# The attention norm's factor spread by a DRAM round trip, later rotary products, and a 128-wide first FoX block

## The chip, the cores and the metric

One Trainium2 chip, one core. The time is that of one execution on the device, in microseconds (us): from the first to the last instruction of the program with what lies around it. The kernel before takes 1466.55 us, the median of three runs (1466.13 to 1466.87).

## The reference, cut to what matters

Two decoder layers on x, 512 tokens of width 1024, all float32. A layer normalizes x by its root mean square, projects it, runs two attention mixers over it (FoX, eight heads with a forget term; NSA, eight heads with compressed, selected and window branches, queries and keys partly rotated), mixes them, and ends in an MLP behind a second norm.

```python
def rmsnorm(x, g):
    y = xf * lax.rsqrt(jnp.mean(xf * xf, axis=-1, keepdims=True) + RMS_EPS)
    return (y * g).astype(x.dtype)
...
    h = rmsnorm(x, norm_mix)
    proj = h @ w_in
    q_a, k_a, v_a, f_a, q_b, kv_b, g_b, gate_a, gate_b = jnp.split(proj, ...)
...
        s = jnp.einsum('bhqd,bhkd->bhqk', qi, k) * scale      # FoX, 128 queries at a time
        s = s + ci[..., :, None] - c[..., None, :]
        s = jnp.where(kpos[None, :] <= qpos[:, None], s, -jnp.inf)
...
    q_n = partial_rope(to_heads(q_b, NSA_HEADS), pos)
    ks = partial_rope(ks, pos)
    kw = partial_rope(kw, pos)
```

## The kernel before, in words

Every product of float32 numbers is made of three matmuls on numbers split into a high and a low part (fp32r): high by high, high by low, low by high. Weights come by DMA from the SyncE queue into `raw`; `convert` (L175 to L192) splits them, the high part `wh` by a copy on ScalarE (L189), the low part `wl` by a subtraction on VectorE (L190). All activations lie transposed, features on the partitions and tokens along the row, and x is multiplied by the norm's gain but not by the norm's factor before the projections. The factor, one number for each token, is put on each projection's result instead. It is needed in two forms:

- `rc`, [128, 4]: the factor of token 128 b + p in partition p, column b. The projections with tokens on the partitions use it (`vf`, L806 and L807; `vn`, `z`, `th`, L819 to L824).
- `R`, [128, 512]: the factors of all 512 tokens along the row, the same in every partition. The projections with tokens along the row use it: `scaled` (L344) for FoX's keys and queries, the two rotary tables `CRS` (L829 to L832), which `roped` (L334 to L340) multiplies with the NSA queries and keys, and the gates (L915).

`rstd` (L266) makes both: four matmuls sum the squares over the partitions (L273), a few small operations of VectorE and ScalarE make `rc` (L276 to L284), then four matmuls of `rc`'s columns with the identity write `R` into a PSUM bank (L289), and ScalarE copies it to SBUF (L294). `layer` (L781) calls it once a layer, between the value projection (`va`) and the second small projection (`g2`), and lets two steps of the projection go between the last small operation and the four matmuls.

In each layer the stages around it are: the value projection and `g2` (`token_proj`, in four chunks of weights each), the forget term (`forget`), the first pair of FoX heads (`fox_proj(0)`), then `attend` over the eight FoX units. A unit's `scores` (L404) makes, for each of four blocks of 128 queries, the scores against the keys up to that block, with two matmuls of 128 queries (L429 and L432); the first block has 128 keys that count and takes 256 columns, `w = max(n, 256)`. Between the units' matmuls stands the work of a generator, `fill1` (the other projections of FoX, the compression, the NSA keys and queries).

The order on each engine comes from a scheduler in the framework: it orders the program's instructions by its own costs and by what they depend on, each engine then takes its list in that order, and waits at an instruction whose inputs are not there. Only the MLP's order is pinned.

Of the kernel before, what the change touches and what calls it, by code (L numbers as in the profile page):

```python
# [19 lines left out]
T = 512  # L20
# [122 lines left out]
class Body:  # L143
# [119 lines left out]

        self.nc.scalar.activation(self.t("s4", [128, 1], name="warm"), after[:, :1], f)

    def rstd(self, acc, tags=("O", "O"), wait=iter(()), exp=True, copy=True):  # L266

        nc = self.nc
        n = acc[0].shape[-1] // 128
        ps = self.p(tags[0])  # L270
        for b in range(n):
            for i, t in enumerate(acc):
                nc.tensor.matmul(ps[:, 2 * b:2 * b + 2], t[:, b * 128:(b + 1) * 128],  # L273
                                 self.ones2, start=i == 0, stop=i == len(acc) - 1)
        v, s, y, z = (self.t("s4", [128, NB], name=k)[:, :n] for k in "vsyz")
        nc.vector.tensor_scalar(v, ps[:, 0:2 * n:2], 1.0 / D, 1e-6, op0=OP.mult, op1=OP.add)  # L276
        nc.scalar.activation(s, v, AF.Sqrt)
        if exp:
            self.table(AF.Exp, s)
        nc.vector.reciprocal(y, s)  # L280
        nc.vector.tensor_mul(z, y, y)
        nc.vector.scalar_tensor_tensor(z, z, -0.5, v, op0=OP.mult, op1=OP.mult)
        rc = self.t("g4", [128, NB], name="rcol")[:, :n]
        nc.vector.scalar_tensor_tensor(rc, z, 1.5, y, op0=OP.add, op1=OP.mult)  # L284
        for _ in range(2):
            next(wait, None)
        ps = self.p(tags[1])[:, :128 * n]
        for b in range(n):
            nc.tensor.matmul(ps[:, b * 128:(b + 1) * 128], rc[:, b:b + 1].to_broadcast([128, 128]), self.ident,  # L289
                             start=True, stop=True)  # L290
        if not copy:
            return ps, rc
        R = self.t("r", [128, T], name="R")[:, :128 * n]
        nc.scalar.copy(R, ps)  # L294
        return R, rc


# [106 lines left out]
    def scores(self, u):  # L404
        nc = self.nc
        q, k = u["q"](), u["k"]()
        E = self.t("e", [128, 1280], name="E")
        sm = u.get("sm")
        if sm is None:
            sm = self.t("s4", [128, NB], name="sm")  # L410
        u["E"] = u.get("E", [])

        def probs(e, ps, sm, i):
            n = 128 * (i + 1)
            mx = self.t("s4", [128, 1], name="mx")
            with self.tc.high_priority(20):
                nc.vector.tensor_tensor_reduce(e, ps, self.mask[:, T - n:], -1.0, BIG, OP.add, OP.min, mx)  # L417
                nc.scalar.activation(e, e, AF.Exp, bias=mx, scale=-1.0, accum_out=sm[:, i:i + 1])  # L418

        for i in range(len(u["E"]), NB):  # L420
            n = 128 * (i + 1)
            w = max(n, 256)
            ps = self.p("S")
            qs = q[:, i * 128:(i + 1) * 128]
            keys = k[:, :, :w]
            mate = u.get("mate") if i == 0 else None
            if mate is not None:
                keys = u["kk"]()
            nc.tensor.matmul(ps[:, :w], qs, keys[:, 0], start=True, stop=False)  # L429
            if "qx" in u:  # L430
                qs = u["qx"]()[:, i * 128:(i + 1) * 128]
            nc.tensor.matmul(ps[:, :w], qs, keys[:, 1], start=False, stop=True)  # L432
            e = E[:, 64 * i * (i + 1):64 * (i + 1) * (i + 2)]
            probs(e, ps[:, :n], sm, i)
            u["E"].append(e)
            if mate is not None:
                e = self.t("e0", [128, 128])
                mate["sm"] = self.t("s4", [128, NB], name="sm")
                probs(e, ps[:, 128:256], mate["sm"], 0)
                mate["E"] = [e]  # L440
            yield
        r = self.t("s4", [128, NB], name="rr")
        nc.vector.reciprocal(r, sm)
        if "gate" in u:
            nc.vector.tensor_mul(r, r, u["gate"]())
        for i in range(NB):
            e = u["E"][i]
            if i > 0:
                nc.vector.tensor_scalar(e, e, r[:, i:i + 1], None, op0=OP.mult)
            else:  # L450
                nc.scalar.activation(e, e, AF.Copy, scale=r[:, i:i + 1])  # L451
# [329 lines left out]
    def layer(self, l, u):  # L781
# [8 lines left out]
        for i in range(6 if l else 8):  # L790
            next(g)
            if l and i == 2:
                self.acc = self.late()
        self.R, self.rc = R, rc = self.rstd(self.acc, ("O", "O"), wait=g)
        if l:
            self.pinned()
        run(g)
# [28 lines left out]
        nc.vector.tensor_scalar(gt, th.rearrange("p b (h c) -> p b c h", c=3), 0.5, 0.5, op0=OP.mult, op1=OP.add)  # L826
        for b in range(NB):
            nc.vector.tensor_scalar(gt[:, b, 0], gt[:, b, 0], self.const("rowv")[:, b:b + 1], None, op0=OP.mult)
        self.CRS = self.t("crs", [128, 2, T])  # L829
        nc.sync.dma_start(self.CRS, a["rope"])  # L830
        for i in range(2):
            nc.vector.tensor_tensor(self.CRS[:, i], self.CRS[:, i], R, op=OP.mult)  # L832
        self.forget(z.rearrange("p b h -> p (b h)"))

        st = {}
# [30 lines left out]
            yield from self.cmp_probs(hk)  # L866

        def fill1():
            yield from fox_proj(1)
            yield from proj(8, "kc", self.scaled)  # L870
            yield from proj(9, "vc", self.scaled)
            c = self.compress(st["kc"], st["vc"], small, l)
            self.kk = self.t("crs", [128, 2, 2, 2, 128], F32R, name="kk")
            rest = chain(fox_proj(2), fox_proj(3), proj(10, "ks", lambda ps: self.k_pair(self.roped(ps), branch=0)),
                         proj(11, "kw", lambda ps: self.k_pair(self.roped(ps), branch=1)), qproj(0), qproj(1))
            yield from alternate(c, rest)
# [220 lines left out]
    def go(self):  # L1097
        nc, a = self.nc, self.a
        self.gain = self.cp.tile([128, 40], F32, name="gain")
        nc.scalar.dma_start(self.gain, a["gain"])  # L1100
        self.ones2 = self.cp.tile([128, 2], F32, name="ones")
        nc.vector.memset(self.ones2, 1.0)
        ones = self.t("tmp", [128, 128], name="ones")
        nc.vector.memset(ones, 1.0)
        ps = self.p("PT")
        for _ in range(self.WARM):
            nc.tensor.matmul(ps[:, :128], ones, ones, start=True, stop=True)
        warm = self.t("s4", [128, 1], name="warm")
        nc.scalar.activation(warm, ones[:, :1], AF.Exp)
        self.xs, self.xr = ([self.dp.tile([128, T], F32, name=f"{n}{k}") for k in range(KT)] for n in ("xs", "xr"))  # L1110
        self.x_src = [a["xT"][k] for k in range(KT)]
        self.acc, u = [], []
        self.plan = deque(x for l in range(L) for x in self.order(l))
        self.loaded, self.split = deque(), deque()
        self.raws = deque(("e", "e"))
        for l in range(L):
            u = self.layer(l, u)
            self.x_src = self.xs
# [703 lines left out]
```

## Time and profile before

| | before |
|---|---|
| median of 3 runs | 1466.55 us (1466.13 to 1466.87) |
| the profiled execution's own time | 1466.06 us |
| its span, first to last instruction | 1464.3 us |
| TensorE (PE) busy | 1450.4 us, 99% |
| VectorE (DVE) busy | 1205.9 us, 82% |
| ScalarE (ACT) busy | 916.7 us, 63% |
| GpSimd (POOL) busy | 146.6 us, 10% |
| granted TensorE clock | 0.998 of 2.4 GHz |

PE is TensorE's matmuls, PEld its weight loads. A matmul's duration in the trace runs over its neighbours (matmuls are pipelined), so what one costs is read from the distance between starts. Layer 0's norm stands near 30 us of the span, layer 1's near 748 us.

### The profile page before, as it was taken

How to read it: one execution, taken by the hardware profiler on the slowest of the kernel's cores; microseconds unless marked ns; L12 is line 12 of the kernel's file. 1: busy time of each engine (PE TensorE's matmuls, PEld its weight loads, DVE VectorE, ACT ScalarE, POOL GpSimd, SP SyncE). 2: the span in 40 equal slices, each digit the busy share in tenths (PEclk: the TensorE clock that was granted, in tenths of full speed). 3: DMA queues.
4: the chain of work that ended last, by engine and by line, in shares of the span. 5: the costliest groups of instructions: out<-in, count | busy, mean ns of one | idle time of the engine just before them, and what ended most of it. 6: DMA issues, size and time to landing. Idle time of an engine off the chain costs nothing.

```text
span 1464.3 us, 23475 instructions
## 1 busy us (share of the span) xinstructions
PE 1450.4 (99%) x8312; PEld 1261.2 (86%) x8312; DVE 1205.9 (82%) x2490; ACT 916.7 (63%) x1886; POOL 146.6 (10%) x199
## 2 busy tenths in 40 slices
PE   9999999999999999999999999999999999999997
PEld 8877888888898999989888788888888989899896
DVE  6587988777789898989866779887787888989897
ACT  6375666664577575848454657666646776757584
POOL 2000100000011111111300001000000111111113
PEclk9999999999999999999999999999999999999999
DMA  7564522126447676777836644221353475766774
GB/s 255 168 158 135 151 87 65 66 73 201 137 113 181 176 175 183 177 171 214 255 133 166 178 114 126 87 72 59 97 177 101 118 176 154 185 176 175 180 192 115
DMA packets 79477, 216.72 MB, mean 148 GB/s; under 512 B 10112, under 2 KB 10496, under 8 KB 79360
## 3 DMA queue, kind: packets, MB, share of 16 engines
q1 hardware_dynamic: 59104, 164.08, 35.3%
q0 software_dynamic: 17664, 46.67, 17.5%
q10 hardware_dynamic: 2592, 4.48, 0.8%
q8 instruction: 65, 1.06, 0.3%
q14 instruction: 52, 0.43, 0.1%
HBM read 168.46 MB, written 6.29 MB: 119 GB/s over the span
## 4 chain that ended last, share of the span: by engine, by line
PE 94%; DVE 3%; ACT 2%; issue 1%; DMA 0%; POOL 0%; ACTq 0%; DVEq 0%
PE ps_mm L215 10%; PE ps_mm L216 10%; PE ps_mm L217 9%; PE ps_mm L1530 7%; PE ps_S L1530 7%; PE ps_mm L1403 6%; PE ps_PT L1403 6%; PE ps_S L1403 6%; PE ps_O L485 4%; PE ps_PT L464 4%; PE ps_O L1403 3%; PE ps_O L1530 3%; PE ps_PT L1530 3%; PE ps_S L429 2%; PE ps_S L432 2%; PE ps_O L575 1%
## 5 line engine op out<-in xcount | busy, mean ns | idle before, releaser
L215 PE MATMUL ps_mm<-uh,wh 128*128 128x512 f32 x480 | 191.3, 398 | 0.2
L216 PE MATMUL ps_mm<-ul,wh 128*128 128x512 f32 x480 | 189.2, 394 | 0.0
L217 PE MATMUL ps_mm<-uh,wl 128*128 128x512 f32 x480 | 188.4, 392 | 0.0
L189 ACT CAST wh<-raw 128x1024 fp32r<-128x1024 f32 (+2 forms) x111 | 112.6, 1015 | 88.1 <-PE ps_mm L216 50.3
L1512 ACT CAST sh<-raw 128x512 fp32r<-128x512 f32 x160 | 96.7, 620 | 78.0 <-DVE raw L1611 26.8
L190 DVE TENSOR_TENSOR wl<-raw,wh 128x1024 fp32r<-128x1024 f32 (+2 forms) x111 | 130.5, 1177 | 17.2 <-ACT wh L189 17.1
L418 ACT ACTIVATE E<-E,mx 128x512 f32<-128x512 f32 (+3 forms) x176 | 101.3, 576 | 48.9 <-DVE mx L417 48.0
L468 ACT CAST pth<-ps_PT 128x512 fp32r<-128x512 f32 x144 | 73.2, 514 | 76.1 <-PE ps_PT L464 75.5
L1520 DVE TENSOR_TENSOR sl<-raw,sh 128x512 fp32r<-128x512 f32 x160 | 106.2, 684 | 12.1 <-ACT sh L1512 11.8
L417 DVE CUSTOM_DVE_ANT_0 E<-ps_S,ct 128x512 f32<-128x512 f32 (+3 forms) x176 | 87.3, 501 | 30.6 <-PE ps_S L432 29.8
L469 DVE TENSOR_TENSOR ptl<-ps_PT,pth 128x512 fp32r<-128x512 f32 x144 | 84.7, 597 | 33.3 <-ACT pth L468 31.8
L217 PEld LDWEIGHTS ps_mm<-uh,wl 128*128 128x128 f32 x480 | 90.2, 188 | 18.5
L215 PEld LDWEIGHTS ps_mm<-uh,wh 128*128 128x128 f32 x480 | 90.3, 188 | 15.6 <-DVE tmp L337 0.8
L216 PEld LDWEIGHTS ps_mm<-ul,wh 128*128 128x128 f32 x480 | 90.4, 188 | 13.6
L1377 POOL DMA_DIRECT2D raw<-raw x32 | 28.0, 874 | 734.8 <-DVE sl L1370 194.5
L1356 ACT CAST sh<-raw 128x512 fp32r<-128x512 f32 x128 | 74.6, 618 | 37.0 <-DMA raw<-raw 29.9
L1370 DVE TENSOR_TENSOR sl<-raw,sh 128x512 fp32r<-128x512 f32 x128 | 84.0, 685 | 10.8 <-ACT sh L1356 10.7
L1403 PE MATMUL ps_S<-t,sh 128*128 128x256 f32 x384 | 83.0, 282 | 0.0
L464 PE MATMUL ps_PT<-ct,E 128*128 128x128 f32 x464 | 76.3, 275 | 0.9 <-ACT E L451 0.6
L1356 ACT CAST sh<-sx 128x512 fp32r<-128x512 f32 x96 | 58.4, 615 | 28.7 <-DVE sx L1338 24.7
L1403 PE MATMUL ps_S<-t,sl 128*128 128x256 f32 x256 | 72.0, 281 | 0.0
L1370 DVE TENSOR_TENSOR sl<-sx,sh 128x512 fp32r<-128x512 f32 x96 | 64.5, 686 | 8.0 <-ACT sh L1356 7.7
(452 smaller groups left out, 4406.4 us busy)
## 6 DMA issues: line engine op xcount, KB each, us to landing
raw<-wb SPq DMA_DIRECT2D x64, 512.0 KB
raw<-wup SPq DMA_DIRECT2D x64, 512.0 KB
raw<-wt POOLq DMA_DIRECT2D x48, 512.0 KB, 6.6
raw<-wt SPq DMA_DIRECT2D x32, 512.0 KB
sx<-wt SPq DMA_DIRECT2D x64, 256.0 KB
kd<-hl SPq DMA_DIRECT2D x40, 256.0 KB
w<-w SPq DMA_DIRECT2D x32, 256.0 KB
raw<-wo SPq DMA_DIRECT2D x16, 512.0 KB
```

Source lines behind the costliest of these rows:

```text
L189: nc.scalar.copy(h[:, :n], raw[:, :n])
L190: nc.vector.tensor_tensor(lo[:, :n], raw[:, :n], h[:, :n].bitcast(F32), op=OP.subtract)
L215: mm(ps, h[:, c], xh, start=start and i == 0, stop=False)
L216: mm(ps, h[:, c], xl, start=False, stop=False)
L217: mm(ps, lo[:, c], xh, start=False, stop=stop and i == ks - 1)
L418: nc.scalar.activation(e, e, AF.Exp, bias=mx, scale=-1.0, accum_out=sm[:, i:i + 1])
L464: nc.tensor.transpose(ps[:, j * 128:(j + 1) * 128], E[i][:, b * 128:(b + 1) * 128], self.ident)
L1356: self.nc.scalar.copy(h, self.source(k, i))
L1370: self.nc.vector.tensor_tensor(lo, self.source(k, i), h.bitcast(F32), op=OP.subtract)
L1403: self.nc.tensor.matmul(ps, w, x, skip_group_check=True, **kw)
L1520: self.nc.vector.tensor_tensor(lo, self.operand(d, i, p), h.bitcast(F32), op=OP.subtract)
L1530: self.nc.tensor.matmul(ps[t][:, cols], a[:, s], m, start=new and f == 0, stop=f == 2, skip_group_check=True)
```

## The change

`rstd` no longer makes `R` with matmuls. It writes `rc` to a small DRAM tile `row` of [4, 128] by a DMA from POOL's queue, turned so that the 512 factors stand in a row, and reads that row back into all 128 partitions of `R` by a second DMA from the same queue. Second, `CRS` is allocated and its two products with `R` are written in `fill1`, the load before FoX's second pair of projections and the products behind it. Third, FoX's first block of scores is 128 columns wide, not 256; NSA's stays at 256.

```diff
@@ rstd @@
-    def rstd(self, acc, tags=("O", "O"), wait=iter(()), exp=True, copy=True):
+    def rstd(self, acc, tag="O", wait=iter(()), exp=True):
...
         nc.vector.scalar_tensor_tensor(rc, z, 1.5, y, op0=OP.add, op1=OP.mult)
+        nc.gpsimd.dma_start(self.row.rearrange("b p -> p b"), rc)
         for _ in range(2):
             next(wait, None)
-        ps = self.p(tags[1])[:, :128 * n]
-        for b in range(n):
-            nc.tensor.matmul(ps[:, b * 128:(b + 1) * 128], rc[:, b:b + 1].to_broadcast([128, 128]), self.ident,
-                             start=True, stop=True)
-        if not copy:
-            return ps, rc
-        R = self.t("r", [128, T], name="R")[:, :128 * n]
-        nc.scalar.copy(R, ps)
+        R = self.t("r", [128, T], name="R")
+        nc.gpsimd.dma_start(R, self.row.rearrange("b p -> (b p)")[None, :].to_broadcast([128, T]))
         return R, rc
@@ scores @@
-            w = max(n, 256)
+            w = max(n, 256) if "qx" not in u else n
@@ layer @@
-        self.CRS = self.t("crs", [128, 2, T])
-        nc.sync.dma_start(self.CRS, a["rope"])
-        for i in range(2):
-            nc.vector.tensor_tensor(self.CRS[:, i], self.CRS[:, i], R, op=OP.mult)
...
         def fill1():
+            self.CRS = self.t("crs", [128, 2, T])
+            nc.sync.dma_start(self.CRS, a["rope"])
             yield from fox_proj(1)
+            for i in range(2):
+                nc.vector.tensor_tensor(self.CRS[:, i], self.CRS[:, i], R, op=OP.mult)
@@ go @@
+        self.row = self.dp.tile([NB, 128], F32, name="row")
```

The scheduler places the moved instructions by itself. On VectorE in layer 0, from the factor `rcol` to the first FoX weights (`wl` of 128x1024), the order before is:

```order
L284 SCALAR_TENSOR_TENSOR rcol<-z,y 128x4
L815 TENSOR_SCALAR rch<-rcol 128x4
L807 SCALAR_TENSOR_TENSOR vf<-ps_PT,rcol,vf 128x8x64
L807 SCALAR_TENSOR_TENSOR vf<-ps_S,rcol,vf 128x8x64
L832 TENSOR_TENSOR crs<-crs,R 128x512
L807 SCALAR_TENSOR_TENSOR vf<-ps_PT,rcol,vf 128x8x64
L807 SCALAR_TENSOR_TENSOR vf<-ps_S,rcol,vf 128x8x64
L190 TENSOR_TENSOR wl<-raw,wh 128x576
L832 TENSOR_TENSOR crs<-crs,R 128x512
L190 TENSOR_TENSOR wl<-raw,wh 128x576
L190 TENSOR_TENSOR wl<-raw,wh 128x1024
```

The same place on VectorE with the change (its line numbers are 4 or 5 lower there, and L864 is the product of the rotary tables):

```order
L284 SCALAR_TENSOR_TENSOR rcol<-z,y 128x4
L810 TENSOR_SCALAR rch<-rcol 128x4
L802 SCALAR_TENSOR_TENSOR vf<-ps_PT,rcol,vf 128x8x64
L802 SCALAR_TENSOR_TENSOR vf<-ps_S,rcol,vf 128x8x64
L190 TENSOR_TENSOR wl<-raw,wh 128x576 x2
L864 TENSOR_TENSOR crs<-crs,R 128x512 x2
L190 TENSOR_TENSOR wl<-raw,wh 128x1024
```

The tables' two products, written behind FoX's second projection, stand together ahead of the first FoX weights: the first has moved behind two `vf` and two `wl`, the second behind one `wl`. In layer 1 they stay where they were, behind the second `wl` of 128x576 and ahead of the last two.

On POOL the two DMAs stand in layer 0 between two of the memsets of FoX's `qx`:

```order
L391 MEMSET qx 64x512
L392 MEMSET qx 2x512
L285 DMA row<-rcol 128x4x1
L289 DMA R<-row 128x512
L391 MEMSET qx 64x512
```

Before, the same memsets follow each other with nothing between them. The SyncE queue keeps its order, the load of the tables among it.

On TensorE the four matmuls of L289 are gone from each layer, and FoX's first blocks are narrower. Where the second pair's scores begin in layer 0 (`q_753` and `q_748` are the same queries under two names), the order before is:

```order
L216 MATMUL ps_mm<-ul,wh 128x512
L429 MATMUL ps_S<-kd,q_753 128x256 x2
L217 MATMUL ps_mm<-uh,wl 128x512
L485 MATMUL ps_O<-pth,vf 128x128
L485 MATMUL ps_O<-ptl,vf 128x128
L215 MATMUL ps_mm<-uh,wh 128x512
```

With the change TensorE has there:

```order
L216 MATMUL ps_mm<-ul,wh 128x512
L217 MATMUL ps_mm<-uh,wl 128x512
L424 MATMUL ps_S<-kd,q_748 128x128
L424 MATMUL ps_S<-kd,q_748 128x256
L480 MATMUL ps_O<-pth,vf 128x128
L480 MATMUL ps_O<-ptl,vf 128x128
L215 MATMUL ps_mm<-uh,wh 128x512
```

The first of the two scores is 128 wide, and one matmul of the projection changes sides. FoX and the first NSA units hold some twenty such moves, by one to a few matmuls each; none leaves its stage.

## Rows read from the trace of the kernel before

**Rows 1.** The page: the span, and the engines' busy time, share and instructions.

```profile
span 1464.3 us, 23475 instructions
PE 1450.4 (99%) x8312; PEld 1261.2 (86%) x8312; DVE 1205.9 (82%) x2490; ACT 916.7 (63%) x1886; POOL 146.6 (10%) x199
```

**Rows 2.** The page: the chain that ended last, by engine.

```profile
PE 94%; DVE 3%; ACT 2%; issue 1%; DMA 0%; POOL 0%; ACTq 0%; DVEq 0%
```

**Rows 3.** Windows: stretch, length, engines' busy time, PE clock, DMA share, GB/s.

```profile
12.00:345.00 333.00, 331.85 (x1759) 276.55 (x1758) 256.61 (x627) 199.85 (x440) 10.45 (x21) 1.00 0.44 128
```

**Rows 4.** Timeline of PE around L289, both layers: start, duration, instruction.

```profile
30.66 1.05 PE L289 MATMUL ps_O<-ct,rcol 128*128 128x128 f32 x8
...
31.68 0.29 PE L324 MATMUL ps_O<-wl,uh 128*128 128x288 f32 x1
...
752.57 1.05 PE L289 MATMUL ps_O<-ct,rcol 128*128 128x128 f32 x8
...
753.59 0.30 PE L324 MATMUL ps_mm<-wl,uh 128*128 128x288 f32 x1
```

**Rows 5.** Timeline of PE: fp32r matmuls of 128 and of 256 columns among wider ones.

```profile
201.28 0.39 PE L217 MATMUL ps_mm<-uh,wl 128*128 128x512 f32 x1
201.51 0.22 PE L485 MATMUL ps_O<-pth,vn 128*128 128x128 f32 x1
201.57 0.28 PE L485 MATMUL ps_O<-ptl,vn 128*128 128x128 f32 x1
201.68 0.45 PE L215 MATMUL ps_mm<-uh,wh 128*128 128x512 f32 x1
201.97 0.39 PE L216 MATMUL ps_mm<-ul,wh 128*128 128x512 f32 x1
...
203.11 0.28 PE L429 MATMUL ps_S<-kk,q 128*128 128x256 f32 x1
...
203.34 0.27 PE L464 MATMUL ps_PT<-ct,e 128*128 128x128 f32 x1
```

**Rows 6.** The line L432: FoX's second matmuls, by width.

```profile
L432 PE MATMUL ps_S<-kd,qx x64: 274/333/423, 68.9 to 881.3; 128*128 128x256 f32 x32, 128*128 128x384 f32 x16, 128*128 128x512 f32 x16
```

**Rows 7.** Timeline of DVE in layer 0, from the factor to the first use of R.

```profile
29.99 0.16 DVE L284 SCALAR_TENSOR_TENSOR rcol<-z,y 128x4 f32<-128x4 f32 x1
...
40.25 1.23 DVE L190 TENSOR_TENSOR wl<-raw,wh 128x1024 fp32r<-128x1024 f32 x1 [2.79 <-ACT wh L189]
...
48.01 0.68 DVE L344 TENSOR_TENSOR tmp<-ps_PT,R 128x512 f32<-128x512 f32 x1
```

**Rows 8.** Timeline of PE: the first matmul that reads the first FoX weights' wl.

```profile
42.61 0.40 PE L217 MATMUL ps_PT<-uh,wl 128*128 128x512 f32 x1
```

**Rows 9.** Timeline of DVE in layer 1: the factor, the tables' products, the next wl.

```profile
748.20 0.16 DVE L284 SCALAR_TENSOR_TENSOR rcol<-z,y 128x4 f32<-128x4 f32 x1
...
754.82 1.28 DVE L832 TENSOR_TENSOR crs<-crs,R 128x512 f32<-128x512 f32 x2
757.56 0.76 DVE L190 TENSOR_TENSOR wl<-raw,wh 128x576 fp32r<-128x576 f32 x1 [1.45 <-ACT wh L189]
```

**Rows 10.** Timeline of PE in layer 1: the first matmul that reads that wl.

```profile
759.96 0.29 PE L324 MATMUL ps_mm<-wl,uh 128*128 128x288 f32 x1
```

**Rows 11.** The lines L365 (64 KB) and L1029 (256 KB), DMAs from POOL's queue.

```profile
DMA to landing us min/median/max: 2.6/3.1/3.3
...
DMA to landing us min/median/max: 3.0/4.0/9.2
```

**Rows 12.** The page: POOL's DMA queue: packets, MB, share of 16 engines' span.

```profile
q0 software_dynamic: 17664, 46.67, 17.5%
```

**Rows 13.** Windows around the place of the new DMAs, columns as in rows 3.

```profile
32.00:34.00 2.00, 2.00 (x17) 2.00 (x17) 2.00 (x4) 1.91 (x4) 0.00 (x0) 1.00 0.00 0
...
752.00:754.00 2.00, 2.00 (x17) 1.89 (x16) 2.00 (x4) 2.00 (x5) 0.00 (x0) 1.00 0.27 99
```

**Rows 14.** Timeline of POOL: its first work in layer 0 after the opening memsets.

```profile
105.47 0.54 POOL L396 MEMSET qx<- 64x512 f32 x1 [97.39 <-PE ps_O L575]
```

More of the change, by code (lines that the diff above doesn't have):

```diff
@@ L264, in table @@
         self.nc.scalar.activation(self.t("s4", [128, 1], name="warm"), after[:, :1], f)
-    def rstd(self, acc, tags=("O", "O"), wait=iter(()), exp=True, copy=True):
+    def rstd(self, acc, tag="O", wait=iter(()), exp=True):
         nc = self.nc
         n = acc[0].shape[-1] // 128
-        ps = self.p(tags[0])
+        ps = self.p(tag)
         for b in range(n):
@@ L793, in layer @@
                 self.acc = self.late()
-        self.R, self.rc = R, rc = self.rstd(self.acc, ("O", "O"), wait=g)
+        self.R, self.rc = R, rc = self.rstd(self.acc, wait=g)
         if l:
```

## The prediction

> **What bounds the kernel now.** I read the page first: TensorE is busy 1450.4 of 1464.3 us [rows 1], and it holds 94% of the chain that ended last [rows 2]. Then the windows: over the whole of layer 0 up to its MLP, 333 us, TensorE lacks 1.2 us [rows 3]. So the time is TensorE's list: what is taken from that list is gained, what is taken from another engine is worth nothing, and a delay elsewhere costs only where it passes its slack and TensorE then stands still. The three edits are therefore read as: what leaves TensorE's list, what becomes cheaper on it, and which wait is new.
>
> **Part 1, the four matmuls that made R.** From the first of them to the second matmul behind them, 30.66 to 31.68 us, is 1.02 us in layer 0, and in layer 1, 752.57 to 753.59, the same [rows 4]. One matmul of 288 columns lies in that stretch; 512 columns take 0.23 us from start to start [rows 5], 288 by their width 0.13. So the R matmuls hold TensorE for 0.89 us in each layer, and their removal gives **-1.8 us**. The copy of R on ScalarE goes too; ScalarE is busy 63% [rows 1] and stood on no path here, so I cost it at nothing. The cover for that is TensorE's list, and if the cover went the copy's end could only be a further gain.
>
> **Part 2, FoX's first block.** Eight heads in two layers, two matmuls each: 32 matmuls go from 256 to 128 columns (the 256-wide ones of L432 number 32, half of them the first block [rows 6], and L429 has as many). The trace has 128-wide matmuls on the same kind of number, fp32r by fp32r: two of them and one of 512 columns take 201.51 to 201.97, 0.46 us, of which 0.23 is the wide one (201.28 to 201.51 is such a distance); so two narrow ones take 0.23 us. Two of 256 columns take 203.11 to 203.34, 0.23 us [rows 5]. Half the width costs the same. I take **0**. The bounds: if the price went with the width, 0.115/2 x 32 = 1.8 us would be gained; if they ran like the float32 matmuls of R, 0.89/4 = 0.22 us each, 0.11 x 32 = 3.4 us would be lost, but the operands here are those of the fp32r rows, which are the nearest, so I leave that end out.
>
> A rule speaks for the other value. The Trainium skill, "TensorE: Matmul & The Clock Gate", section "Back-to-back issue gap", lists 134 cycles for 128 columns and 262 for 256, which at the full clock (1.00 in rows 3) would be 53 ns less for each matmul; by it this part would give 1.7 us, and the rows disagree with it. That stands as a rival below.
>
> **Part 3, R by way of DRAM.** The new wait is on VectorE. The products of the rotary tables with R stand ahead of a conversion of weights in VectorE's list, in layer 0 ahead of the first FoX weights' `wl`, in layer 1 ahead of the third `wl` of the small projection. VectorE takes its list in order, so until R has landed nothing behind the products runs: that `wl`, then `z`, `vn`, the gates and the forget term. TensorE waits for the `wl` first. Let D be the time from the end of `rcol` to R's landing.
>
> - Layer 0: `rcol` ends at 29.99 + 0.16 = 30.15 [rows 7]. TensorE first reads the `wl` at 42.61 [rows 8], which moves to 41.72 with 0.89 us gone ahead of it. Back from there: 1.23 for the `wl` [rows 7] and 1.28 for the two products [rows 9] leave 39.21. So D may be 9.1 us.
> - Layer 1: `rcol` ends at 748.36, TensorE first reads the `wl` at 759.96 [rows 10], moved to 759.07; less 0.76 and 1.28 [rows 9] is 757.03. So D may be 8.7 us.
>
> What D is: the trace has no such pair. It is bounded by POOL's own DMAs: 64 KB land 2.6 to 3.3 us after issue, median 3.1, and 256 KB, R's size, 3.0 to 9.2, median 4.0 [rows 11]. The second waits for the first, so the sum: 5.6 at the least, 7.1 by the medians, 12.5 at the most. The write has one thing that none of these has, 512 pieces of 4 bytes. On POOL's queue a packet takes 0.175 x 16 x 1464.3 / 17664 = 0.23 us on average [rows 12], most of it bytes; 32 pieces on each of 16 engines at that price would be 7.4 us, so the far upper end is 19.9. A piece of 4 bytes has nearly no bytes, so I take an eighth of it, 0.9, and D = 8.0. The DMA engines are idle at 32 to 34 us and 27% busy at 752 to 754 [rows 13], which is for the medians and not for 9.2. At 8.0 both layers keep 0.7 to 1.1 us of slack: **0**. Each microsecond of D beyond 9.1 costs one in each layer.
>
> The Trainium skill, "DMA: Bandwidth & Descriptors", section "Rules for kernel authors", says that a last dimension that is not contiguous goes as one descriptor per element and should be avoided; that is this write, it speaks against the change, and no row shows its price. Its section "Anatomy of one DMA" has 2.0 us + bytes/436e3 for a DMA from POOL, by which D would be an estimated 4.6 us and the sum the same.
>
> **The smaller moves.** R's other uses begin at 48.01 in layer 0 [rows 7], about 10 us behind R's landing, so they wait for nothing at D = 8. POOL now waits at its second DMA for the first; behind it in layer 0 stands a memset that began at 105.47 [rows 14], so nobody waits for that. SyncE's list is unchanged: the tables are loaded where they were. The `wl`, the exponentials and the score matmuls that change places in FoX and in the first NSA units do so by a few matmuls of 0.23 us; TensorE has to issue the same list, and its idle time there is the 1.2 us [rows 3]. I give these ±0.5 us.
>
> **The sum.** -1.8 + 0 + 0 = -1.8 us. Against the profiled execution, 1466.06 us in all with 1.8 us around the span, 1464.3 becomes 1462.5 and 1466.06 becomes 1464.3. That execution is 0.5 us under the median of the runs, so as a median I predict **1464.8 us**, 0.12% less. A measurement of this kernel can tell about 0.2% (2.9 us) from no change, and this lies within.
>
> **Rivals.**
>
> - *R lands late, and the kernel is slower.* Place: VectorE at the tables' products, for R; then TensorE for the `wl` behind them. Price: (D - 9.1) + (D - 8.7). It has eaten the 1.8 us at D = 9.8, is slower by more than 2.9 us from D = 11.3, and at D = 12.5 (the two worst landings) gives 3.4 + 3.8 - 1.8 = +5.4, 1472.0 us. At the far end, 19.9, it would be 10.8 + 11.2 - 1.8 = +20, 1487. For it: 9.2 us has been seen for 256 KB, and the 4-byte pieces are unknown. Against: idle DMA engines at the place. Chance of over +2.9 us: 0.14. Between D = 8.7 and 11.3 the time lies from 1464.8 to 1469.5, chance 0.16, no change that can be told.
> - *Narrow matmuls are cheaper after all.* If the price goes with the width, part 2 gives 1.8 us, and the sum is -3.6, 1462.9 us, faster by 0.25%. For it: in the rows wide matmuls do go by width, 0.23 for 512 and 0.115 for 256. Against: the narrow ones in rows 5. It is the gap table named above. Chance 0.10.
> - *The change does not shorten TensorE's list.* The 0.89 us are refilled: TensorE comes sooner to weights that are not split yet and waits there. For it: VectorE idled 2.79 us for ScalarE ahead of the first FoX `wl` [rows 7], so conversions follow TensorE's releases of buffers. Against: those releases come sooner as well, since they are TensorE's own. Then 1466.5 us, chance 0.06.
>
> **How the numbers follow.** My forecast with D up to 8.7 has 0.54, within 0.2% but for a tail of 0.02 on the fast side. Faster by over 0.2%: 0.10 + 0.02 = 0.12. Slower: 0.14. Within: 0.74. The predicted time is the likeliest case's. The range reaches below to the narrow-matmul rival, 1462.8, and above to D = 11.5, where 2.4 + 2.8 - 1.8 gives 1469.9: 1462.8 to 1470.0. What is left out is mostly the later landings, some 0.13, and 0.03 below.
>
> **What would show it.** Right: no L289 matmuls on TensorE and 1.8 us less span; on POOL's two new lines landings of about 4 us each; VectorE going into the tables' products with a short wait or none, and TensorE with no idle time at 41 to 43 and 757 to 760 us; starts of FoX's 128-wide matmuls 0.115 us apart. Wrong: VectorE idle at L864 with a DMA as the releaser, beyond 39.2 or 757.0 us, and TensorE idle for DVE `wl` behind it; or starts of 0.06 us after the narrow matmuls and a neighbour that is no later; or new idle time on TensorE in FoX, which no row of before has.

## The result: 1482.8 us, 16.5 us more than before, and the profile after

| | before, same chip | changed |
|---|---|---|
| median of 4 runs | 1466.34 us (1465.73 to 1466.87) | 1482.84 us (1481.84 to 1485.69) |
| ratio, 95% interval | 1 | 1.0115 [1.0103, 1.0128] |
| profiled execution, span | 1466.06 us, 1464.3 us | 1485.69 us, 1483.9 us |

The change is slower by 1.15%, outside the predicted range of 1462.8 to 1470.0. The profiled execution is the longest of the four, 2.9 us over their median; the readings below are its own. From the page, the span, the engines and the head of the chain that ended last:

```profile
span 1483.9 us, 23447 instructions
PE 1455.1 (98%) x8296; PEld 1264.6 (85%) x8296; DVE 1206.4 (81%) x2490; ACT 915.3 (62%) x1884; POOL 147.9 (10%) x203
...
PE 89%; issue 3%; DMA 2%; DVE 2%; ACT 2%; POOL 1%; SPq 0%; DVEq 0%; POOLq 0%; ACTq 0%
```

Beside [rows 1, 2], TensorE is busy 4.7 us longer although matmuls were taken from its list, and its share of the chain falls from 94% to 89%. DMA (0% to 2%), POOL (0% to 1%) and issue time (1% to 3%) come onto the chain; VectorE and ScalarE had 3% and 2% of it before and have 2% each now. POOL's two new transfers, in the timeline of its issues (layer 0, then layer 1), and in the view of DMA issues of layer 0, whose last column is the time from issue to landing:

```profile
30.41 0.98 POOL L285 DMA_DIRECT2D row<-rcol  x1 [22.34 <-DVE rch L810]
41.49 0.56 POOL L289 DMA_DIRECT2D R<-row  x1 [10.11 <-DMA row<-rcol]
...
758.91 0.78 POOL L285 DMA_DIRECT2D row<-rcol  x1 [18.84 <-DVE rch L810]
768.84 0.55 POOL L289 DMA_DIRECT2D R<-row  x1 [9.15 <-DMA row<-rcol]
...
R<-row POOLq DMA_DIRECT2D x1, 256.0 KB, 5.6
row<-rcol POOLq DMA_DIRECT2D x1, 2.0 KB, 10.8
```

POOL stands 10.11 and 9.15 us between the two: the write of 2 KB takes that long. VectorE's timeline, layer 0 and layer 1 (beside [rows 7, 9]):

```profile
29.92 0.16 DVE L284 SCALAR_TENSOR_TENSOR rcol<-z,y 128x4 f32<-128x4 f32 x1
...
35.75 0.76 DVE L190 TENSOR_TENSOR wl<-raw,wh 128x576 fp32r<-128x576 f32 x1 [1.26 <-ACT wh L189]
47.12 1.29 DVE L864 TENSOR_TENSOR crs<-crs,R 128x512 f32<-128x512 f32 x2 [10.61 <-DMA R<-row]
48.33 1.22 DVE L190 TENSOR_TENSOR wl<-raw,wh 128x1024 fp32r<-128x1024 f32 x1
...
758.46 0.16 DVE L284 SCALAR_TENSOR_TENSOR rcol<-z,y 128x4 f32<-128x4 f32 x1
...
774.15 1.29 DVE L864 TENSOR_TENSOR crs<-crs,R 128x512 f32<-128x512 f32 x2 [8.98 <-DMA R<-row]
775.36 1.42 DVE L190 TENSOR_TENSOR wl<-raw,wh 128x576 fp32r<-128x576 f32 x2
```

VectorE stands 10.61 and 8.98 us at the tables' products, and the `wl` behind them starts at 48.33, where it started at 40.25 before [rows 7]. D, from the end of `rcol` to the start of the products that wait for R, is 47.12 - 30.08 = 17.0 us and 774.15 - 758.62 = 15.5 us. TensorE's timeline there:

```profile
41.07 0.29 PE L320 MATMUL ps_O<-wh,ul 128*128 128x288 f32 x1
44.84 0.64 PE L215 MATMUL ps_PT<-uh,wh 128*128 128x512 f32 x1 [3.47 <-ACT wh L189]
45.27 0.63 PE L216 MATMUL ps_PT<-ul,wh 128*128 128x512 f32 x1
49.60 0.80 PE L217 MATMUL ps_PT<-uh,wl 128*128 128x512 f32 x1 [3.70 <-DVE wl L190]
...
54.89 0.58 PE L217 MATMUL ps_PT<-uh,wl 128*128 128x512 f32 x1
55.31 0.40 PE L215 MATMUL ps_PT<-uh,wh 128*128 128x512 f32 x1
55.54 0.39 PE L216 MATMUL ps_PT<-ul,wh 128*128 128x512 f32 x1
...
772.31 0.61 PE L318 MATMUL ps_mm<-wh,uh 128*128 128x288 f32 x1 [2.96 <-ACT wh L189]
776.17 0.61 PE L319 MATMUL ps_mm<-wl,uh 128*128 128x288 f32 x1 [3.25 <-DVE wl L190]
```

Two waits in each layer: one for `wl`, which the prediction named as a rival, and ahead of it one for `wh`, which it did not name. For `wh`, ScalarE in turn waited for the weights' DMA. SyncE's issue of the load of FoX's first weights and ScalarE's conversion of them, with the change:

```profile
34.52 0.33 SPq L173 DMA_DIRECT2D raw<-wb  x1
...
43.74 1.04 ACT L189 CAST wh<-raw 128x1024 fp32r<-128x1024 f32 x1 [8.02 <-DMA raw<-wb]
```

And before:

```profile
35.18 0.33 SPq L173 DMA_DIRECT2D raw<-wb  x1
...
39.17 1.05 ACT L189 CAST wh<-raw 128x1024 fp32r<-128x1024 f32 x1 [2.51 <-PE ps_O L325]
```

The load was issued no later than before, and came some 9 us after its issue, where before it was there within 4. The third effect stands in the windows (columns: window, length, then busy time and instructions of PE, PEld, DVE, ACT and POOL, granted clock, share of the DMA engines' time, GB/s):

```profile
34.00:36.00 2.00, 2.00 (x17) 2.00 (x16) 0.74 (x2) 0.67 (x1) 0.00 (x0) 1.00 1.94 59
36.00:38.00 2.00, 2.00 (x17) 2.00 (x16) 0.51 (x1) 0.00 (x0) 0.00 (x0) 1.00 0.39 10
38.00:40.00 2.00, 2.00 (x17) 2.00 (x16) 0.00 (x0) 0.00 (x0) 0.00 (x0) 1.00 0.75 41
40.00:42.00 2.00, 1.37 (x11) 1.13 (x9) 0.00 (x0) 0.00 (x0) 0.51 (x1) 1.00 0.28 27
42.00:44.00 2.00, 0.00 (x0) 0.00 (x0) 0.00 (x0) 0.26 (x1) 0.05 (x1) 1.00 0.95 381
...
48.00:50.00 2.00, 0.40 (x1) 0.40 (x2) 2.00 (x6) 0.28 (x2) 0.00 (x0) 0.50 0.00 0
50.00:52.00 2.00, 2.00 (x6) 1.52 (x6) 1.64 (x6) 2.00 (x10) 0.00 (x0) 0.50 0.71 244
52.00:54.00 2.00, 2.00 (x6) 1.56 (x5) 2.00 (x8) 1.02 (x2) 0.00 (x0) 0.50 0.05 18
```

While the write is under way the DMA engines move 10 to 59 GB/s (262 and 238 before, over 36 to 40 us) at a share that reads between 0.39 and 1.94. A share over 1 cannot be occupied time, so it is no proof that the engines are full. In the window from 42 to 44 us, behind the write, they move 381 GB/s, the queued weight load of 512 KB among it. And TensorE, having stood idle from 41.4 to 44.8 and from 45.9 to 49.6, runs at a granted clock of 0.50, its lower level of 1.2 GHz, up to 55 us: from 49.60 to 55.31 there are 13 matmuls in 5.71 us, 0.44 each, and behind that 0.23.

Layer 0 adds up when it is read from start to start. The same places before:

```profile
42.02 0.30 PE L325 MATMUL ps_O<-wh,ul 128*128 128x288 f32 x1
42.15 0.39 PE L215 MATMUL ps_PT<-uh,wh 128*128 128x512 f32 x1
...
45.58 0.39 PE L215 MATMUL ps_PT<-uh,wh 128*128 128x512 f32 x1
```

The last matmul of the small projection comes 0.95 us earlier (42.02, now 41.07), as R's matmuls are gone. From it to FoX's first matmul are 3.77 us in place of 0.13, from there to the first `wl` matmul 4.76 in place of 0.46 [rows 8], and the next 13 matmuls take 5.71 in place of 2.97. That is 3.64 + 4.30 + 2.74 - 0.95 = 9.73 us, and FoX's first score matmul moved from 66.58 to 76.33 us, by 9.75: no later wait took any of it back. Layer 1 starts 10.3 us later (its first transposes 726.31 before, 736.58 now), and its first score matmul comes 19.1 us later (790.63, 809.70), so layer 1 loses another 8.8. The remaining 1.0 us of the profiled execution's 19.6 lies elsewhere and is not assigned.

### The profile page after: what moved, and what is told of

It is laid out like the page before. It is cut to its first block, busy times and chain, and to the rows that moved or that the text cites. A ratio compares the mean times of both kernels' runs of the same rounds, so it can differ in the third digit from the quotient of the medians.

```text
span 1483.9 us, 23447 instructions
## 1 busy us (share of the span) xinstructions
PE 1455.1 (98%) x8296; PEld 1264.6 (85%) x8296; DVE 1206.4 (81%) x2490; ACT 915.3 (62%) x1884; POOL 147.9 (10%) x203
## 4 chain that ended last, share of the span: by engine, by line
PE 89%; issue 3%; DMA 2%; DVE 2%; ACT 2%; POOL 1%; SPq 0%; DVEq 0%; POOLq 0%; ACTq 0%
PE ps_mm L215 10%; PE ps_mm L216 9%; PE ps_mm L217 9%; PE ps_mm L1526 7%; PE ps_S L1526 7%; PE ps_S L1399 6%; PE ps_mm L1399 6%; PE ps_PT L1399 6%; PE ps_O L480 4%; PE ps_PT L459 3%; PE ps_O L1526 3%; PE ps_PT L1526 3%; PE ps_O L1399 3%; PE ps_S L424 2%; PE ps_S L427 2%
## 5 line engine op out<-in xcount | busy, mean ns | idle before, releaser
L1366 DVE TENSOR_TENSOR sl<-raw,sh 128x512 fp32r<-128x512 f32 x128 | 84.0, 687 | 10.8 <-ACT sh L1352 10.8
```

Of the source, the lines that this page charges most:

```text
L1366: self.nc.vector.tensor_tensor(lo, self.source(k, i), h.bitcast(F32), op=OP.subtract)
```

## The experiments

Theory A: R's lateness stops VectorE at the products, and TensorE behind it. Theory B: the write of 512 pieces of 4 bytes holds up the weight loads. Theory C: the fall of the clock behind the stall is a loss of its own. The kernel before was run beside each on the same chip, with medians of 1466.34 to 1467.53 us.

**The dead write: theory B by itself.** The kernel before with one instruction more in each layer:

```diff
+            nc.gpsimd.dma_start(self.row.rearrange("b p -> p b"), rc)
```

> The kernel before, with the element-by-element write of the factor (512 pieces of 4 bytes per layer) added behind `rcol`; nobody reads it, R is still made by matmuls. Theory A (only R's lateness costs): nobody waits for the write, 1466 us, within 0.2% of before. Theory B (the write keeps the DMA engines from the weight loads queued behind it): `wh` of the projections waits for `raw` as in the changed kernel (3.0 and 3.5 us of PE waits there), so 1466 + 6.5 = 1473 us, and up to 1479 if TensorE's clock falls to 1.2 GHz behind those waits as it does in the changed kernel (2.9 us per layer).

Measured 1475.39 us, ratio 1.0063 [1.0048, 1.0078]. A write that nobody reads costs 8.8 us. It landed after 11.1 and 9.5 us, and TensorE's waits for `wh` were (total us, times, longest; layer 0, then layer 1):

```profile
PE ps_PT L215 <- ACT wh L189: 2.3, 1, 2.3
PE ps_mm L325 <- ACT wh L189: 1.9, 1, 1.9
```

The waits are shorter than expected (4.2 us, with 0.9 for `wl`), and the clock fell in layer 0 alone, where it cost some 1.6 us (0.50 and 0.70 over 46 to 50 us). By starts, 4.4 us are lost up to layer 0's first scores and 2.8 between layer 1's start and its first scores; some 1.6 lie elsewhere and are not assigned. Theory B is right, and A is not all.

**Four rows in place of the pieces.**

```diff
-        nc.gpsimd.dma_start(self.row.rearrange("b p -> p b"), rc)
+        pt = self.p(tag)
+        nc.tensor.transpose(pt[:n, :128], rc, self.ident)
+        rt = self.t("tmp", [128, T], name="rt")[:n, :128]
+        nc.scalar.copy(rt, pt[:n, :128])
+        nc.gpsimd.dma_start(self.row, rt)
```

> The changed kernel, but the factor is turned by one transpose on TensorE and written to HBM as four rows of 512 bytes in place of 512 pieces of 4 bytes; the broadcast read is unchanged. Theories A and B both say that the pieces are at fault: the write lands in about 2.6 to 3.1 us as other small issues of POOL do, R is there 3 + 5.4 us plus 1 to 2 us for the transpose behind `rcol`, some 10 to 11 us against a slack of 9, and no load is held up: 1465 to 1472 us. Theory D (it is the round trip of two transfers, whatever their pieces): 1480 us or more.

Measured 1467.98 us, 1.0008 [0.9999, 1.0018]. The same 2 KB landed in 1.8 and 1.6 us, R's read in 4.1, VectorE waits 1.1 us for R in one layer, and TensorE waits for no weights; its one new wait of over 1 us is for `rcol` at the transpose, 1.4 us in layer 1. The round trip itself costs no more than a measurement can tell; the pieces are at fault.

**The same with the transpose later**, behind the two steps of projection that R's matmuls stood behind:

```diff
-        pt = self.p(tag)
...
-        nc.gpsimd.dma_start(self.row, rt)
         for _ in range(2):
             next(wait, None)
+        pt = self.p(tag)
...
+        nc.gpsimd.dma_start(self.row, rt)
```

> As the kernel with four rows of 512 bytes, with the transpose behind the two steps of projection that the matmuls of R stood behind in the kernel before. TensorE stood 1.4 us for `rcol` at the transpose in layer 1 there and the clock fell to 0.73 behind it in the stretch 750 to 755 us of the trace with three more copies; here both should go: 1468.0 - 1.4 - 1 = 1465.6 us, 1464 to 1467. If the wait is no part of the path: 1468 us again.

Measured 1466.30 us, 0.9998 [0.9990, 1.0007]. TensorE's wait for `rcol` went, the time came down by 1.5 us (each kernel against its own before) where 2.4 were expected, and the kernel is level with the one before, not ahead of it.

**R late without a 4-byte piece.** Three copies of the 2 KB from HBM to HBM follow the four rows:

```diff
+        for i in range(3):
+            nc.gpsimd.dma_start(self.hop[i + 1], self.hop[i])
```

> As the kernel with four rows of 512 bytes, with three further copies of the 2 KB from HBM to HBM between the write and the broadcast read, so that R comes about as late as in the changed kernel (3 x 2.6 us = 8 us later than with the rows alone) without a single 4-byte piece. Theory A (R's lateness stops VectorE at the table products and TensorE behind it): 7 us of PE waits per layer and the clock's fall again, 1480 to 1488 us. Theory B alone (the loads held up by the pieces cost the time, R's lateness is hidden behind them): no load is late, within 3 us of the kernel with four rows.

Measured 1467.05 us, 1.0002 [0.9992, 1.0012], against theory A as put. R was as late as asked for, but the scheduler, which knows of the copies, put the products further back on VectorE:

```profile
44.50 1.23 DVE L190 TENSOR_TENSOR wl<-raw,wh 128x1024 fp32r<-128x1024 f32 x1
45.65 0.35 DVE L724 RECIPROCAL f<-f 128x32 f32<-128x32 f32 x1
46.10 0.69 DVE L870 TENSOR_TENSOR crs<-crs,R 128x512 f32<-128x512 f32 x1
```

Two conversions of FoX's weights now stand ahead of the products. R 16 us behind `rcol` costs nothing if nothing that TensorE needs stands behind the products. So the experiment was made again with the order forced, the products tied ahead of the first conversion:

```diff
+        if str(src) == self.spot:
...
+            for i in range(2):
+                nc.vector.tensor_tensor(self.CRS[:, i], self.CRS[:, i], self.R, op=OP.mult)
+            nc.vector.tensor_copy(lo[:, :1], self.CRS[:, 0, :1])
         nc.vector.tensor_tensor(lo[:, :n], raw[:, :n], h[:, :n].bitcast(F32), op=OP.subtract)
```

> The kernel with four rows of 512 bytes and three more copies (R lands about 16 us behind `rcol`, no 4-byte piece), with the products of the rotary tables forced ahead of the conversion of FoX's first weights on VectorE. Theory A (VectorE standing at the products is enough): TensorE waits for `wl` from the last gate projection at 41 us to about 48.6 us, 7 us per layer, and its clock falls behind it: 1479 to 1484 us; the held-up loads of the changed kernel then lie inside a wait that R's lateness makes anyway. If the two causes add up (16.5 in all, 8.9 of it from the pieces): 1466.5 + 7.5 = 1474 us.

Measured 1476.59 us, 1.0063 [1.0048, 1.0078]: 9.7 us over the kernel before, where the kernel without the forced order was 0.5 over its own. TensorE in layer 0:

```profile
43.71 0.50 PE L222 MATMUL ps_PT<-uh,wh 128*128 128x512 f32 x1 [1.88 <-ACT wh L189]
44.04 0.40 PE L223 MATMUL ps_PT<-ul,wh 128*128 128x512 f32 x1
48.10 0.79 PE L224 MATMUL ps_PT<-uh,wl 128*128 128x512 f32 x1 [3.66 <-DVE wl L196]
```

The new waits for weights are all in layer 0; in layer 1 the tied conversion comes late enough, and TensorE waits for no weights there. That is why the total is below the 1479 to 1484 expected, which counted both layers, though above the rival's 1474. In the layer that it reached, theory A by itself brings as much as the whole change lost there: first scores at 76.03 us, 76.33 in the changed kernel. No load is held up: ScalarE waits for no weights' DMA there, and the 1.88 us stand at the second chunk's weights, of which TensorE takes two matmuls early in this order.

**The write kept, the products later.** The changed kernel with the products tied behind the first scaled projection:

```diff
-                nc.vector.tensor_tensor(self.CRS[:, i], self.CRS[:, i], R, op=OP.mult)
+                nc.vector.scalar_tensor_tensor(self.CRS[:, i], self.CRS[:, i], self.one, R, op0=OP.mult, op1=OP.mult)
```

> The changed kernel, its 512-piece write included, with the products of the rotary tables tied to the first scaled projection, so that VectorE comes to them only after the conversions of FoX's first weights. Theory A alone (VectorE standing at the products costs the time): 1466 us. Theories A and B together: the `wl` wait on TensorE (3.2 and 3.7 us) goes and the `wh` wait (3.0 and 3.5 us) stays, with a shorter fall of the clock: about what the dead write cost, 1473 to 1477 us. If neither is the cause, 1482 us again.

Measured 1475.44 us, 1.0060 [1.0046, 1.0074]: the dead write's time. TensorE's waits for `wl` are 0.6 us in all, those for `wh` 6.0. So the change has two causes that run side by side: the held-up loads alone cost 8.8 us, and R's lateness brings the total to 16.5. The two overlap and do not add: in layer 0 R's lateness alone ends where both together end (76.03 and 76.33 us), so there R, the later of them, sets the end.

**The other parts of the change.** FoX's first block alone, and with it the later products while R stays with matmuls:

```diff
-            w = max(n, 256)
+            w = max(n, 256) if "qx" not in u else n
```

> The kernel before with FoX's first block 128 wide as the only edit. The prediction's step (128 columns cost TensorE what 256 cost, and the softmax beside it is hidden): no difference, 1466.5 us within 0.1%. Rival (half the columns, half the time): 32 matmuls x 0.058 us = 1.8 us less, 1464.7 us.

The changed kernel with R by matmuls:

```diff
-        nc.gpsimd.dma_start(self.row.rearrange("b p -> p b"), rc)
...
+            nc.tensor.matmul(ps[:, b * 128:(b + 1) * 128], rc[:, b:b + 1].to_broadcast([128, 128]), self.ident,
+                             start=True, stop=True)
...
-        nc.gpsimd.dma_start(R, self.row.rearrange("b p -> (b p)")[None, :].to_broadcast([128, T]))
+        nc.scalar.copy(R, ps)
```

> The changed kernel with R made by matmuls again, so that only the later products and the 128-wide block are left of the change. If the whole loss is in the spread through HBM: 1466.5 us within 0.15%, no PE wait of 3 us at the projections. If the later place of the table load or of the products costs by itself: a PE wait for `wl` or `wh` at FoX's first projection remains, and 1470 us or more.

Measured 1465.37 us, 0.9992 [0.9983, 1.0001], and 1465.28 us, 0.9993 [0.9985, 1.0002]. Neither can be told from no change, and no loss is left without the spread. The spread alone on the kernel before, with the products at their old place in the program:

```diff
+        nc.gpsimd.dma_start(self.row.rearrange("b p -> p b"), rc)
...
-        nc.scalar.copy(R, ps)
+        nc.gpsimd.dma_start(R, self.row.rearrange("b p -> (b p)")[None, :].to_broadcast([128, T]))
```

> The kernel before with R spread through HBM as in the changed kernel, the table products at their old place and the first block 256 wide. The products then stand on VectorE between the splits of the values and the conversions of the gate projection's weights; with R 17 us late these wait too, and TensorE stands from about 36 us to 49 us: 12 us and more per layer, 1490 to 1500 us. If the place of the products doesn't matter: 1483 to 1485 us.

Measured 1483.09 us, 1.0110 [1.0095, 1.0125]. The expectation of 1490 and more missed: the scheduler had put the products behind the same conversions as in the changed kernel (VectorE waits for R 10.55 us, up to 46.68), so their place in the program decided nothing.

**The clock.** The aim was to fill the stall with 28 matmuls that nobody reads:

```diff
+        fill = self.p("PT")
+        for _ in range(28):
+            nc.tensor.matmul(fill, u[0][0][:, :128], u[0][0], start=True, stop=True)
-        run(fox_proj(0, ("PT", "PT")))
+        with self.tc.high_priority(300):                  # second attempt, and its comparison
+            run(fox_proj(0, ("PT", "PT")))
```

In the first kernel the fillers stood in layer 0's stall, but the forget gate's matmul was drawn ahead and TensorE waited 7.5 us for it; in the second most of them were put behind the stall. Both say nothing on theory C.

> The changed kernel with 28 matmuls of 128x512 added per layer between the last gate projection and FoX's first projection, whose result nobody reads; they fill 28 x 0.227 = 6.4 us of the 7 us for which TensorE stands there. Theory C (about 2.9 us per layer of the loss is TensorE at 1.2 GHz behind the stall): the granted clock stays at 1.00 over 40 to 60 us and 765 to 790 us, and the time falls by 2 x 2.5 to 2 x 2.9 us, from 1482.8 to 1477 to 1478 us. Rival (the clock's fall lies in a stretch that waits anyway, or the fillers only push the work back): 1482 us or more.

> As the kernel with the raised priority, with 28 matmuls of 128x512 more per layer that fill 6.4 of the 7 us for which TensorE stands ahead of those projections, so that the forget gate's matmul no longer stands ahead of them as in the first kernel with fillers. Theory C (TensorE's fall to 1.2 GHz behind the stall costs about 2.9 us per layer): the granted clock stays at 1.00 there and the time is 5 to 6 us under the kernel with the priority alone, 1477 us. Rival (the slow stretch waits for the weights anyway): no difference, within 1.5 us.

> The changed kernel with FoX's first projections raised in the scheduler's priority and nothing else: the comparison for the next kernel. No wait is touched: 1482.8 us within 2 us.

Measured 1498.26 us, 1.0219 [1.0204, 1.0234]; 1498.24 us, 1.0205 [1.0190, 1.0220]; 1484.94 us, 1.0118 [1.0103, 1.0133]. In the third attempt the gate's matmul was tied to the first projection's result, without and with fillers:

```diff
+        nc.vector.tensor_scalar(one, x[:, :1], 0.0, 1.0, op0=OP.mult, op1=OP.add)
...
-        nc.tensor.matmul(ps, wide[:, 1], self.ones2[:, :1].to_broadcast([128, 128]), start=True, stop=False)
+        nc.tensor.matmul(ps, wide[:, 1], one.to_broadcast([128, 128]), start=True, stop=False)
```

> The changed kernel with the forget gate's matmul tied to the first scaled projection (nine operations of one column on VectorE), the comparison for the next kernel: 1482.8 us within 2 us.

> As the kernel with the tied gate, with 28 matmuls of 128x512 more per layer that stand ahead of FoX's first projection, inside the stall. Theory C (the fall to 1.2 GHz behind the stall is time lost): TensorE is busy up to 47.6 us, the granted clock stays at 1.00 or falls for less, 2 to 6 us under the kernel without them. Rival (the slow stretch would have waited anyway): within 1 us of it.

Measured 1482.28 us, 1.0100 [1.0083, 1.0117], and 1492.50 us, 1.0174 [1.0159, 1.0189]. The sum is no verdict either: in layer 1 the fillers stood behind the stall and cost their 6.5 us, and in layer 0 a new wait of 2.82 us for the gate ate the gain, with the clock lower again behind it (0.62 over 60 to 64 us). But layer 0 can be read. Without, and then with fillers:

```profile
49.64 0.80 PE L217 MATMUL ps_PT<-uh,wl 128*128 128x512 f32 x1 [3.52 <-DVE wl L190]
62.01 0.46 PE L737 MATMUL ps_S<-one,fb 128*128 128x128 f32 x2
```

```profile
41.24 6.53 PE L879 MATMUL ps_PT<-uh 128*128 128x512 f32 x28
48.64 0.50 PE L217 MATMUL ps_PT<-uh,wl 128*128 128x512 f32 x1 [0.42 <-DVE wl L190]
60.84 0.67 PE L737 MATMUL ps_S<-one,fb 128*128 128x128 f32 x2 [2.82 <-DVE one L735]
```

With the stall filled the granted clock stayed at 1.00 up to 60 us. From the first `wl` matmul to the gate it took 60.84 - 2.82 - 48.64 = 9.4 us, against 12.4; two matmuls fewer stand between, 0.45 us, so about 2.5 us a layer is the clock. This is read from one trace of each; no total shows it.

**What makes the pieces dear.** All four are the kernel before with a dead write, and differ only in its pieces:

```diff
+            nc.gpsimd.dma_start(self.row, rc)                                        # 128 of 16 bytes
+            nc.gpsimd.dma_start(row.rearrange("b p -> p b"), rc)                     # twice, 1024 of 4
+            nc.gpsimd.dma_start(self.row[:1].rearrange("b p -> p b"), rc[:, :1])     # 128 of 4
+            nc.gpsimd.dma_start(self.row[:, :, 0].rearrange("b p -> p b"), rc)       # 512 of 4, 64 bytes apart
```

> The kernel before with a write of the factor that nobody reads, as with the dead write, but laid out so that each partition's four values are one piece: 128 pieces of 16 bytes per layer in place of 512 of 4 bytes, the same 2 KB. If the loads are held up by the number of pieces: the write lands in 2.6 + 8/4 = 4.6 us, the loads come 2 us later at most, no PE wait for `wh` at the projections: 1466 to 1467.5 us. If by any write of POOL's queue at this place: 1475 us as with 512 pieces.

> The kernel before with the dead write of 512 pieces of 4 bytes issued twice per layer, to two places (1024 pieces). If the pieces go through one after the other and the loads behind them: the second lands some 8 us after the first, TensorE's waits for `wh` grow by 8 us per layer, and its fall of clock lasts longer: 1475.4 + 16 = 1491 us, 1486 to 1497. If the two writes overlap or the loads slip in between them: 1475 to 1480 us.

> The kernel before with a dead write of the factor's first column only: 128 pieces of 4 bytes per layer, side by side in HBM. If a piece of 4 bytes is slow by its size, whatever the count (side by side or not): landing near 10 us and 1475 us as with 512. If the count decides: landing near that of 128 pieces of 16 bytes (2.8 and 1.7 us), 1466.5 us.

> The kernel before with a dead write of 512 pieces of 4 bytes per layer that lie 64 bytes apart in HBM in place of side by side. If pieces that share a stretch of HBM hold each other up: landing falls to 3 to 5 us, no PE wait for `wh`, 1466.5 to 1468 us. If it is the count or the size of the pieces: 10 us and 1475 us again.

| pieces, layout in HBM | landing in layer 0, 1 | time | ratio, 95% interval |
|---|---|---|---|
| 512 of 4 bytes, side by side | 11.1, 9.5 us | 1475.39 us | 1.0063 [1.0048, 1.0078] |
| 1024 of 4 bytes, side by side, two places | 10.5, 9.6 us (medians of the two) | 1477.54 us | 1.0068 [1.0053, 1.0083] |
| 128 of 4 bytes, side by side | 8.0, 8.5 us | 1470.66 us | 1.0027 [1.0015, 1.0038] |
| 128 of 16 bytes, side by side | 2.8, 1.7 us | 1466.30 us | 0.9992 [0.9982, 1.0002] |
| 512 of 4 bytes, 64 bytes apart | 2.4, 2.2 us | 1466.62 us | 1.0002 [0.9992, 1.0011] |

The windows of 36 to 42 us, of the dead write and of the one with its pieces apart:

```profile
36.00:42.00 6.00, 5.76 (x44) 5.53 (x42) 0.76 (x1) 0.12 (x1) 0.00 (x0) 1.00 0.79 74
```

```profile
36.00:42.00 6.00, 6.00 (x48) 6.00 (x47) 2.29 (x4) 2.00 (x4) 0.00 (x0) 1.00 0.53 178
```

Neither the count nor the size of 4 bytes is the price by itself: the same 512 pieces land in 2.4 us and hold up nothing when they lie 64 bytes apart. Nor is lying side by side by itself: pieces of 16 bytes that do land in 2.8 us. It takes both, pieces of 4 bytes from different partitions that lie side by side in HBM. Then the DMA engines move 74 GB/s over these six microseconds and the loads beside the write crawl, where 178 GB/s go through with the pieces apart. What happens in the memory or the engines is not shown, nor at which size or distance it ends. The count has a part as well: 128 pieces of 4 bytes cost 4.3 us, between the two values expected, about half of what 512 cost. The doubled write costs 10.0 us over its own before, against 8.8 for the single one, which fits two writes that run beside each other. A spread that writes its pieces apart was not tried: the broadcast read would then have to gather single elements.

No version beats the kernel before by more than a measurement can tell.

## Why the prediction was wrong

- **The step that failed** is the term for the pieces in Part 3: "A piece of 4 bytes has nearly no bytes, so I take an eighth of it, 0.9". The write was taken at 3.1 + 0.9 = 4.0 us and landed in 10.8 us in layer 0; the whole upper end for the pieces, 3.1 + 7.4 = 10.5, would have come out near it, by luck: it goes by the count of pieces, and the same count 64 bytes apart landed in 2.4. The price was looked for in bytes and packets, and lies in small pieces side by side. The rule of the Trainium skill, "DMA: Bandwidth & Descriptors", section "Rules for kernel authors", spoke against this write, and the runs agree with it for pieces side by side (8.8 us) and not for pieces 64 bytes apart (no difference).
- The read was taken at 4.0 us and took 5.6 in layer 0; with POOL's waits and issues D became 17.0 and 15.5 instead of 8.0. It is inside the far end of 19.9 and beyond the two worst landings, 12.5.
- **The mechanism was the first rival**, with the right place: VectorE at L864, then TensorE for `wl`. Its formula with the measured D gives (17.0 - 9.1) + (15.5 - 8.7) - 1.8 = +12.9. Both D are read from the profiled execution, so the sum is set against that one: 1466.06 + 12.9 = 1479.0 us, and 1485.69 was measured, 6.7 more. It was given 0.14, because idle DMA engines [rows 13] were held for evidence on the write.
- **Two effects had no term.** D was costed as R's lateness alone; that the write would also keep SyncE's weight loads from the DMA engines was left out (8.8 us by itself, side by side with R's lateness). And a stall was priced at its length; the clock's lower level behind it adds about 2.5 us a layer, 5 of the 6.7 us that the formula lacks.
- **Right:** Part 2. In the kernel with this edit alone two 128-wide matmuls and the one of 512 columns behind them take 0.46 us (70.61 to 71.07), and so do two of 256 and one of 512 (71.76 to 72.22); the narrow ones start 0.06 apart, but the one behind the 512 is later by that much:

```profile
70.61 0.22 PE L429 MATMUL ps_S<-kd,q 128*128 128x128 f32 x1
...
71.07 0.39 PE L216 MATMUL ps_mm<-ul,wh 128*128 128x512 f32 x1
...
71.76 0.28 PE L429 MATMUL ps_S<-kd,q 128*128 128x256 f32 x1
...
72.22 0.40 PE L217 MATMUL ps_mm<-uh,wl 128*128 128x512 f32 x1
```

The rival of narrow matmuls is out by these distances. The total does not decide it: 0.9992 [0.9983, 1.0001] is -2.5 to +0.1 us, which holds the predicted 0 and the rival's -1.8.
- **Right but not seen in the total:** R's matmuls are gone from TensorE. Where the spread cost nothing, in the kernel with four rows and the later transpose, the 1.8 us did not show: 0.9998 [0.9990, 1.0007]. A transpose a layer and a new wait of 0.7 us for `wl` are part of what took them back; the rest was not found.

## What to carry to other kernels

Price a small write by how its pieces lie in HBM, not by its bytes: 4-byte pieces of different partitions side by side took 10 us where the same pieces apart, or rows of 512 bytes, took about 2, and weight loads of another queue waited too. Before something with an uncertain arrival goes into an engine's list, look at what stands behind it: R 16 us late was free in one order and cost over 9 us in the other. And where TensorE is the bound, a stall can cost more than its length: behind the two waits of layer 0 here, 7.2 us in all, the granted clock stood at 0.50 and took about 2.5 us more.

## What the runs showed of the hardware that was not expected

- 512 pieces of 4 bytes side by side: 11.1 us to land; 64 bytes apart: 2.4 us; and 128 pieces of 16 bytes side by side: 2.8 us.
- A write of 2 KB on POOL's queue held up weight loads of SyncE's queue: ScalarE waited 6.8 us for FoX's first weights in layer 0 and 6.65 us for the second small projection's in layer 1 in the kernel with the dead write, and for neither with the pieces apart.
- Behind waits of 3.5 and 3.7 us in layer 0 of the changed kernel, TensorE's granted clock was 0.50 for the next 5.7 us of dense matmuls, and then 1.00 again. Behind 1.9 and 0.4 us in layer 1 of the kernel with the dead write it stayed at 1.00.
